# Three tiles of their own for the modulation weights during the output projection of a hybrid mLSTM/GDN block

## The chip, the cores and the metric

The kernel runs on one NeuronCore of a Trainium2 chip. The metric is the device time of one execution in microseconds (us). TensorE is the matrix engine (PE in the profile, its weight loads PEld), VectorE is DVE, ScalarE is ACT, GpSimd is POOL, and SyncE (SP) issues most of the transfers from HBM.

## The reference

One encoder layer on 256 tokens of width 2048, in float32. Only the middle of it matters here:

```
mod = silu(c) @ ada_w + ada_b            # 6 vectors of 2048: shift/scale/gate for mixer and FFN
h   = rms_norm(x) * (1 + scale_m) + shift_m
...                                       # mLSTM branch y_a, gated delta rule branch y_b
x   = x + gate_m * ((g_a * y_a + g_b * y_b) @ w_out)        # the output projection
hf  = rms_norm(x) * (1 + scale_f) + shift_f
gt, up = split(hf @ w_gate_up)
x   = x + gate_f * ((silu(gt) * up) @ w_down)
return rms_norm(x)
```

`w_out` is 2048 x 2048 (16 MiB). `ada_w` is 2048 x 12288, six parts of 16 MiB. Part 4 (`scale_f`) has to be known before the FFN's input can be made, part 5 (`gate_f`) only at the very end.

## The kernel before

Everything is one instruction stream per engine, scheduled ahead of time; an engine runs its instructions in that order, and waits on semaphores for what an instruction needs. The instructions of SP are DMA issues, and an issue that waits holds up all issues behind it.

Weights stream in as tiles of 1 MiB (128 partitions x 8 KB). `tjob` (line 167) is the worker of a dense product: for each of its chunks `u` it takes a tile `raw_...` and loads it (line 177), and then, in two halves of two 128-row blocks each, ACT rounds it into `wh` (line 180), DVE subtracts to get the remainder `wl` (line 181), and TensorE does twelve matmuls of 128x512 per half: eight with `wh` (lines 198 and 199) and four with `wl` (line 201). `wh` and `wl` have three buffers each, so DVE and ACT can be up to three halves ahead of TensorE.

The output projection is four jobs `o0` to `o3` of four chunks each, 32 halves in all, at the loop on lines 1122 to 1139. Names read so: `raw_o1_2` is chunk 2 of job o1, `wl_o1_2_0` the remainder of its first half. After each job `residual` (line 1080) multiplies the two result tiles by `gm` (line 1083), adds them to `x1` (line 1084) and squares them for the norm (line 1085). `gm` itself is made at the start of the stage by `row` (line 1066): DVE builds diagonal tiles `dg` (line 1072), TensorE multiplies them with ones (line 1074), ACT copies the result (line 1075). The stage before is the job `ya3` of `y_a`, whose end adds into `mg` (line 1003) and transposes it into `mgh`/`mgl` (lines 1009 and 242). `x1` is loaded with 2 MiB from ACT's queue at the start of the stage (line 1064).

The modulation vectors are not matmuls. `ada_part` (line 118) is a generator: each step takes a tile `ada{part}_{b}`, loads 1 MiB of `ada_w` into it (line 123) and lets DVE multiply it with the broadcast `silu(c)` and sum it up (line 124). The steps are laid in between other work as `background`; `sums()` advances it by one step. In the output projection the steps of part 4 from `ada4_3` to `ada4_15` are taken: 13 tiles.

Pools: `st` lives through the whole program. Its tag `raw` has three buffers of 8 KB, and both the weights' tiles (line 176) and the `ada` tiles (line 122) take their turns in it: a load into one of them waits until the last reader of the tile three turns earlier is done, which for a weight tile is its second `wl` (line 181) and for an `ada` tile its sum (line 124). `wp` (line 1062) is a pool that lives only in the output projection; it holds `gm`, `dg` and the residual's `tm`, in memory that the pool `ml` of the stages before has given back and that `ffh`/`ffl` of the FFN take afterwards.

Of the kernel before, what the change touches and what calls it, by code (L numbers as in the profile page):

```python
# [9 lines left out]
F32 = mybir.dt.float32  # L10
# [5 lines left out]
P = 128  # L16
T = 256
D = 2048
# [34 lines left out]
def hybrid_block(ctx: ExitStack, tc: tile.TileContext, xr, nfr, crow, pk_d, cst_d, ada2, ada4, win0, winb, wint, wba, wbb, wo, wgu, wd, out, dbg=None):  # L53
# [3 lines left out]
    def pool(stack, name, bufs=1, **kw):  # L57
        return stack.enter_context(tc.tile_pool(name=name, bufs=bufs, **kw))

    cp = pool(ctx, "cp")  # L60
    st = pool(ctx, "st")
# [53 lines left out]
        order(S.activation(row_c[:, g * 512 : (g + 1) * 512], pc_, AF.Silu))  # L115


    def ada_part(part, row_c):

        c0 = part * KB  # L120
        for b in range(KB):
            raw = st.tile([P, D], F32, tag="raw", bufs=3, name=f"ada{part}_{b}")
            nc.sync.dma_start(raw, ada4[part - 2, b])
            V.scalar_tensor_tensor(raw, raw, 1.0, row_c[:, :D], ALU.mult, ALU.mult, accum_out=mod[:, c0 + b : c0 + b + 1])  # L124
            yield True
        V.tensor_tensor(mod[:, c0 : c0 + KB], mod[:, c0 : c0 + KB], pk[:, PK_ADAB + c0 : PK_ADAB + c0 + KB], ALU.add)
        yield True
# [312 lines left out]
    with ExitStack() as s0:  # L440
# [18 lines left out]
        def loads(b):  # L459
            ra = [w0.tile([P, D + 2], F32, tag="ra", bufs=5, name=f"ra{b}_{i}") for i in range(2)]  # L460
            raw = st.tile([P, N0, P], F32, tag="raw", bufs=3, name=f"raw0_{b}")
            for i in range(2):
                order(nc.sync.dma_start(ra[i], ada2[b, :, i]))
            order(nc.sync.dma_start(raw, win0[b]))
            return ra, raw
# [10 lines left out]
        ra, raw = loads(0)  # L476
# [18 lines left out]
        for b in range(KB):  # L495
            if b:
                ra, raw = loads(b)
# [347 lines left out]
    for part in (2, 3, 4):  # L845
        background.append(ada_part(part, row_c))
# [213 lines left out]
    sd.close()  # L1060
    xp = pool(ctx, "xp", side="right")
    wp = pool(sw, "wp")
    x1 = xp.tile([P, 2, D], F32, name="x1")
    S.dma_start(x1, xr)

# [74 lines left out]
    if dbg is not None and "x1" in dbg:  # L1140
        G.dma_start(dbg["x1"], x1)
    background.append(ada_part(5, row_c))
    sw.close()
    sc.close()
    pool(ctx, "edgeF").tile([P, 56], F32, name="edgeF")
# [61 lines left out]
    for j in range(FB // 4):  # L1207
# [4 lines left out]
        for e2 in range(2):  # L1212
            px = gps(f"pxf{j}_{e2}")
            for e in range(2):
                f = 2 * e2 + e
                for t in range(2):
                    PE.transpose(px[:, e * T + t * P : e * T + (t + 1) * P], sg[:, t, f * P : (f + 1) * P], ident)
            b = 4 * j + 2 * e2
# [143 lines left out]
```

## Time and profile before

| | us |
|---|---|
| median of three runs | 2047.38 (2047.14 to 2054.85) |
| the profiled execution, its own time | 2052.6 |
| its span, first to last instruction | 2050.5 |
| TensorE busy | 1963.4 (96% of the span) |
| DVE busy | 1394.8 (68%) |
| ACT busy | 1047.7 (51%) |
| stage of the output projection, first matmul of o0 to the start of the last half of o3 | 1220.09 to 1321.84 |

All starts are in us from the span's beginning. A matmul's busy time is its latency, and matmuls overlap in the array, so where TensorE keeps up is read from the distance of their starts and not from busy time. A row of the timeline ends, in brackets, with how long its engine sat idle before it and what ended that. In the rows of waits the three numbers are us in total, times, and the longest.

### The profile page before, as it was taken

To read this page: it belongs to the slowest core of one execution; us is meant where nothing else is said; L and a number is where in the kernel's file an instruction comes from. 1 tells how busy PE (TensorE), PEld (TensorE's weight loads), DVE (VectorE), ACT (ScalarE), POOL (GpSimd) and SP (SyncE) were. 2 spreads that over 40 slices of the span, in tenths; PEclk is the share of its full clock that TensorE was granted. 3 is DMA by queue.
4 is the path that set the end of the run, shared out by engine and by line. 5 is a ranking of instruction groups with operands and counts; after the bars stand their busy time and mean duration, and the time that the engine had idled before them with its cause. 6 is when DMAs were issued, how large, how long until landed. Compare 5 with 4: busy or idle time off the path is not lost.

```text
span 2050.5 us, 27063 instructions
## 1 busy us (share of the span) xinstructions
PE 1963.4 (96%) x10374; PEld 1711.0 (83%) x10374; DVE 1394.8 (68%) x2059; ACT 1047.7 (51%) x1582; POOL 106.4 (5%) x205
## 2 busy tenths in 40 slices
PE   8999999999999899999999998899999999999998
PEld 6887879988989788889878887678888888888886
DVE  5788776777888588765667777766656665555554
ACT  3147548755774667556443443464444444444443
POOL 0002210110101011101100000000000000000000
PEclk9999999999999999999999999999999999999999
DMA  9986664556667565766986677756766766555553
GB/s 400 420 323 214 194 202 155 179 183 226 235 216 227 180 214 213 236 234 248 368 298 229 218 261 286 279 189 242 259 236 253 254 230 225 197 204 201 202 203 142
DMA packets 78962, 485.64 MB, mean 237 GB/s; under 512 B 10585, under 2 KB 15969, under 8 KB 24433
## 3 DMA queue, kind: packets, MB, share of 16 engines
q1 hardware_dynamic: 63360, 450.95, 60.6%
q0 software_dynamic: 8160, 17.88, 3.8%
q10 hardware_dynamic: 7314, 15.10, 1.9%
q8 instruction: 81, 1.33, 0.3%
q14 instruction: 47, 0.39, 0.1%
HBM read 467.07 MB, written 16.82 MB: 236 GB/s over the span
## 4 chain that ended last, share of the span: by engine, by line
PE 67%; DVE 13%; DMA 11%; ACT 6%; issue 3%; POOL 1%; ACTq 0%; SPq 0%; DVEq 0%; POOLq 0%
PE acc_b L159 4%; PE acc_up L199 4%; PE acc_up L201 4%; PE acc_up L198 4%; PE acc_d L199 4%; PE acc_d L201 4%; PE acc_d L198 4%; PE acc_gt L199 4%; PE acc_gt L201 3%; PE acc_gt L198 3%; DMA ra<-ada 3%; PE acc_b L161 2%; DMA ada<-ada 1%; PE acc_yb L199 1%; PE acc_yb L201 1%
## 5 line engine op out<-in xcount | busy, mean ns | idle before, releaser
L181 DVE TENSOR_TENSOR wl_d<-raw_d,wh_d 128x1024 fp32r<-128x1024 f32 x88 | 107.5, 1225 | 105.3 <-ACT wh_d L180 103.1
L181 DVE TENSOR_TENSOR wl_up<-raw_up,wh_up 128x1024 fp32r<-128x1024 f32 x88 | 107.6, 1225 | 100.0 <-ACT wh_up L180 100.0
L124 DVE SCALAR_TENSOR_TENSOR ada<-ada,crow 128x2048 f32<-128x2048 f32 x64 | 146.4, 2287 | 19.5 <-DMA ada<-ada 19.4
L180 ACT ACTIVATE wh_d<-raw_d 128x1024 fp32r<-128x1024 f32 x88 | 92.9, 1056 | 124.5 <-PE acc_d L199 114.3
L181 DVE TENSOR_TENSOR wl_gt<-raw_gt,wh_gt 128x1024 fp32r<-128x1024 f32 x88 | 107.7, 1224 | 70.1 <-ACT wh_gt L180 68.6
L180 ACT ACTIVATE wh_up<-raw_up 128x1024 fp32r<-128x1024 f32 x88 | 92.9, 1056 | 119.9 <-PE acc_up L199 71.6
L159 PE MATMUL acc_b<-hh,wh_b 128*128 128x256 f32 x576 | 141.4, 288 | 9.3 <-ACT wh_b L155 7.7
L180 ACT ACTIVATE wh_gt<-raw_gt 128x1024 fp32r<-128x1024 f32 x88 | 92.9, 1055 | 108.7 <-PE acc_gt L199 61.3
L159 PE MATMUL acc_b<-hl,wh_b 128*128 128x256 f32 x576 | 138.9, 284 | 0.0
L199 PE MATMUL acc_gt<-wh_gt,hfl 128*128 128x512 f32 x352 | 136.3, 387 | 0.1
L198 PE MATMUL acc_gt<-wh_gt,hfh 128*128 128x512 f32 x352 | 135.2, 384 | 0.0
L199 PE MATMUL acc_up<-wh_up,hfl 128*128 128x512 f32 x352 | 133.6, 379 | 0.0
L198 PE MATMUL acc_up<-wh_up,hfh 128*128 128x512 f32 x352 | 133.5, 379 | 0.0
L198 PE MATMUL acc_d<-wh_d,ffh 128*128 128x512 f32 x344 | 130.8, 380 | 0.0
L199 PE MATMUL acc_d<-wh_d,ffl 128*128 128x512 f32 x344 | 130.7, 380 | 0.0
L159 PEld LDWEIGHTS acc_b<-hh,wh_b 128*128 128x128 f32 x576 | 114.4, 199 | 10.1 <-ACT wh_b L155 8.4
L509 PE MATMUL first<-x,raw 128*128 128x256 f32 x512 | 114.5, 382 | 7.7 <-ACT x L502 7.7
L509 PEld LDWEIGHTS first<-x,raw 128*128 128x128 f32 x512 | 96.2, 190 | 26.0 <-ACT x L502 13.7
L159 PEld LDWEIGHTS acc_b<-hl,wh_b 128*128 128x128 f32 x576 | 114.4, 199 | 0.0
L180 ACT ACTIVATE wh_o<-raw_o 128x1024 fp32r<-128x1024 f32 x64 | 66.2, 1054 | 77.1 <-DMA raw_o<-wo 44.9
L298 DVE SCALAR_TENSOR_TENSOR cv<-pad,pk,cv 128x256 f32<-128x256 f32 x192 | 90.8, 481 | 19.2 <-ACT cv L296 17.1
L156 DVE TENSOR_TENSOR wl_b<-raw_b,wh_b 128x1024 fp32r<-128x1024 f32 x72 | 86.8, 1219 | 24.6 <-ACT wh_b L155 24.2
(369 smaller groups left out, 5031.5 us busy)
## 6 DMA issues: line engine op xcount, KB each, us to landing
ada<-ada SPq DMA_DIRECT2D x64, 1024.0 KB, 4.9
raw_gt<-wgu SPq DMA_DIRECT2D x44, 1024.0 KB, 5.0
raw_up<-wgu SPq DMA_DIRECT2D x44, 1024.0 KB, 5.0
raw_d<-wd SPq DMA_DIRECT2D x44, 1024.0 KB, 4.9
raw_b<-winb SPq DMA_DIRECT2D x36, 1024.0 KB, 5.1
ra<-ada SPq DMA_DIRECT2D x32, 1025.0 KB, 15.7
raw<-win SPq DMA_DIRECT2D x16, 1024.0 KB, 14.5
raw_z<-wint SPq DMA_DIRECT2D x16, 1024.0 KB, 5.1
```

Of the source, the lines that this page charges most:

```text
L124: V.scalar_tensor_tensor(raw, raw, 1.0, row_c[:, :D], ALU.mult, ALU.mult, accum_out=mod[:, c0 + b : c0 + b + 1])
L156: V.tensor_tensor(wl, raw[:, k0 : k0 + 8], wh.bitcast(F32), ALU.subtract)
L159: PE.matmul(o, wh[:, k], both(x, k0 + k).rearrange("p a b -> p b a"), start=k0 + k + i == 0, stop=False)
L161: PE.matmul(o, wl[:, k], both(hh, k0 + k).rearrange("p a b -> p b a"), start=False, stop=k0 + k == KB - 1)
L180: order(S.activation(wh, raws[u][:, k0 : k0 + 2], AF.Copy), early)
L181: order(V.tensor_tensor(wl, raws[u][:, k0 : k0 + 2], wh.bitcast(F32), ALU.subtract), early)
L198: order(PE.matmul(ps[t], tok(xh, kk, t), turns(wh[:, k]), start=kk == 0, stop=False), early and steps > 1)
L199: PE.matmul(ps[t], tok(xl, kk, t), turns(wh[:, k]), start=False, stop=False)
L201: PE.matmul(ps[t], tok(xh, kk, t), turns(wl[:, k]), start=False, stop=kk == last)
L298: V.scalar_tensor_tensor(cv, pd[:, i : i + T], w[i], cv, ALU.mult, ALU.add)
L509: PE.matmul(first[o], raw[:, o], x[:, b], start=b == 0 and o % 2 == 0, stop=b == KB - 1 and o % 2 == 1)
```

## The change

`ada_part` no longer names its pool, tag and number of buffers, but reads them from a list of three. The list says `st`, `raw`, 3 as before, except from the opening of `wp` to its closing, where it says `wp`, `ada`, 3.

```
+    ada_in = [st, "raw", 3]
+
     def ada_part(part, row_c):
...
-            raw = st.tile([P, D], F32, tag="raw", bufs=3, name=f"ada{part}_{b}")
+            raw = ada_in[0].tile([P, D], F32, tag=ada_in[1], bufs=ada_in[2], name=f"ada{part}_{b}")
...
     wp = pool(sw, "wp")
+    ada_in[:] = [wp, "ada", 3]
     x1 = xp.tile([P, 2, D], F32, name="x1")
...
     background.append(ada_part(5, row_c))
+    ada_in[:] = [st, "raw", 3]
     sw.close()
```

The numbers of instructions on each engine stay the same. The scheduler lays some of them in another order, all of it between the end of `ya3` and the start of `o3`; POOL's order does not change. The three new tiles lie in memory that `ml` used (for `mkq`, `vt`, `sgo`, `bc` and `mdec`), and the first load into them, `ada4_3`, now waits for the last addition into `mg` of job `ya3` (line 1003); the next two loads wait for nothing more.

SP at the start of the output projection, before (the number behind a name is the buffer's):

```order
L177 DMA raw_o0_2_10908<-wo 128x2048
L123 DMA ada4_3_10926<-ada4 128x2048
L177 DMA raw_o0_3_10945<-wo 128x2048
L123 DMA ada4_4_10963<-ada4 128x2048
L123 DMA ada4_5_10990<-ada4 128x2048
L177 DMA raw_o1_0_10995<-wo 128x2048
L123 DMA ada4_6_11029<-ada4 128x2048
```

SP at the same place, now (line numbers are two higher here):

```order
L179 DMA raw_o0_2_10908<-wo 128x2048
L179 DMA raw_o0_3_10945<-wo 128x2048
L125 DMA ada4_3_10926<-ada4 128x2048
L125 DMA ada4_4_10963<-ada4 128x2048
L125 DMA ada4_5_10990<-ada4 128x2048
L179 DMA raw_o1_0_10995<-wo 128x2048
L125 DMA ada4_6_11029<-ada4 128x2048
```

`raw_o0_3` went ahead of `ada4_3`. From `raw_o1_0` on, the order of issues is that of before (a weight tile, an `ada` tile in turn); what an issue waits for is another tile.

DVE around the end of job o0, before (L181 makes `wl`, L124 sums an `ada` tile, L1083 and L1084 are the residual):

```order
L181 TENSOR_TENSOR wl_o0_3_2_10967<-raw_o0_3_10945,wh_o0_3_2_10966 128x1024
L124 SCALAR_TENSOR_TENSOR ada4_5_10990,mod_85<-ada4_5_10990,crow_73 128x2048
L181 TENSOR_TENSOR wl_o1_0_0_10998<-raw_o1_0_10995,wh_o1_0_0_10997 128x1024
L1083 TENSOR_TENSOR tmss1_10835_0_0_10982<-acc_o0_0_10838,gm_10802 128x512
L1083 TENSOR_TENSOR tmss1_10835_1_0_10986<-acc_o0_1_10839,gm_10802 128x512
L1084 TENSOR_TENSOR x1_10800<-x1_10800,tmss1_10835_0_0_10982 128x512
L1084 TENSOR_TENSOR x1_10800<-x1_10800,tmss1_10835_1_0_10986 128x512
L181 TENSOR_TENSOR wl_o1_0_2_11014<-raw_o1_0_10995,wh_o1_0_2_11013 128x1024
L124 SCALAR_TENSOR_TENSOR ada4_6_11029,mod_85<-ada4_6_11029,crow_73 128x2048
L181 TENSOR_TENSOR wl_o1_1_0_11035<-raw_o1_1_11032,wh_o1_1_0_11034 128x1024
```

DVE at the same place, now (line numbers are two to three higher):

```order
L183 TENSOR_TENSOR wl_o0_3_2_10967<-raw_o0_3_10945,wh_o0_3_2_10966 128x1024
L126 SCALAR_TENSOR_TENSOR ada4_6_11029,mod_85<-ada4_6_11029,crow_73 128x2048
L183 TENSOR_TENSOR wl_o1_0_0_10998<-raw_o1_0_10995,wh_o1_0_0_10997 128x1024
L183 TENSOR_TENSOR wl_o1_0_2_11014<-raw_o1_0_10995,wh_o1_0_2_11013 128x1024
L1086 TENSOR_TENSOR tmss1_10835_0_0_10982<-acc_o0_0_10838,gm_10802 128x512
L1086 TENSOR_TENSOR tmss1_10835_1_0_10986<-acc_o0_1_10839,gm_10802 128x512
L1087 TENSOR_TENSOR x1_10800<-x1_10800,tmss1_10835_0_0_10982 128x512
L1087 TENSOR_TENSOR x1_10800<-x1_10800,tmss1_10835_1_0_10986 128x512
L183 TENSOR_TENSOR wl_o1_1_0_11035<-raw_o1_1_11032,wh_o1_1_0_11034 128x1024
L126 SCALAR_TENSOR_TENSOR ada4_7_11050,mod_85<-ada4_7_11050,crow_73 128x2048
```

The residual of o0 now stands behind both `wl` of the next job's first chunk and not behind one; the sums of the `ada` tiles stand one step earlier. At the end of o1 it stands behind two `wl` where it stood behind none, and at the end of o2 behind one where it stood behind none. Near the start of the stage the sum of `ada4_3` moved behind the diagonals `dg2_2`, `dg2_3` and both `mgl`; it now stands right ahead of `wl_o0_1_2`.

More of the change, by code (lines that the diff above doesn't have):

```diff
@@ L115, in c_row @@
         order(S.activation(row_c[:, g * 512 : (g + 1) * 512], pc_, AF.Silu))
+    ada_in = [st, "raw", 3]
     def ada_part(part, row_c):
@@ L121, in ada_part @@
         for b in range(KB):
-            raw = st.tile([P, D], F32, tag="raw", bufs=3, name=f"ada{part}_{b}")
+            raw = ada_in[0].tile([P, D], F32, tag=ada_in[1], bufs=ada_in[2], name=f"ada{part}_{b}")
             nc.sync.dma_start(raw, ada4[part - 2, b])
@@ L1062, in hybrid_block @@
     wp = pool(sw, "wp")
+    ada_in[:] = [wp, "ada", 3]
     x1 = xp.tile([P, 2, D], F32, name="x1")
@@ L1142, in hybrid_block @@
     background.append(ada_part(5, row_c))
+    ada_in[:] = [st, "raw", 3]
     sw.close()
```

## The prediction

> **What bounds the kernel now.** I read the page's busy times first, then the stage in question by windows, then its waits, then TensorE's and DVE's timelines. TensorE leads over the whole program and two thirds of the chain that ends last run on it:
>
> ```profile
> PE 1963.4 (96%) x10374; PEld 1711.0 (83%) x10374; DVE 1394.8 (68%) x2059; ACT 1047.7 (51%) x1582; POOL 106.4 (5%) x205
> PE 67%; DVE 13%; DMA 11%; ACT 6%; issue 3%; POOL 1%; ACTq 0%; SPq 0%; DVEq 0%; POOLq 0%
> ```
>
> So a transfer or a DVE wait costs time only where TensorE runs dry. Three windows (the columns are length, busy times of PE, PEld, DVE, ACT, POOL, granted clock, DMA share, GB/s): a stretch near the start in which transfers are queued deep, the last stretch of `ya3`, and the output projection.
>
> ```profile
> 25.00:50.00 25.00, 22.97 (x105) 19.30 (x104) 16.28 (x18) 3.21 (x8) 0.00 (x0) 1.00 1.01 420
> 1201.69:1220.09 18.40, 18.40 (x87) 16.12 (x86) 9.99 (x11) 7.80 (x9) 0.00 (x0) 1.00 0.49 171
> 1223.50:1321.50 98.00, 86.59 (x370) 70.70 (x369) 76.33 (x89) 37.22 (x49) 0.00 (x0) 0.97 0.84 313
> ```
>
> `ya3` keeps TensorE full; the output projection does not, although none of DVE, ACT and the DMA engines is full either. Who waits there (stretch 1200 to 1325, then SP's own waits in 1180 to 1330):
>
> ```profile
> ACT wh_o L180 <- DMA raw_o<-wo: 44.9, 10, 8.5
> PE acc_o L198 <- ACT wh_o L180: 8.2, 5, 3.5
> PE acc_o L201 <- DVE wl_o L181: 3.2, 3, 1.8
> ...
> SPq L123 <- DVE wl_o L181: 46.9, 13, 8.1
> SPq L177 <- DVE ada L124: 34.4, 13, 8.0
> ```
>
> This is a loop through the shared ring of three tiles: a weight tile's load is held until DVE has summed an `ada` tile (13 times), the `ada` load until DVE has made a `wl` (13 times), and then ACT waits ten times for a weight tile that was issued too late. TensorE's timeline gives what this costs. Starts of halves, and the gaps in them:
>
> ```profile
> 1220.09 0.38 PE L198 MATMUL acc_o<-wh_o,mgh 128*128 128x512 f32 x1
> ...
> 1232.70 0.38 PE L198 MATMUL acc_o<-wh_o,mgh 128*128 128x512 f32 x1
> ...
> 1235.29 0.38 PE L198 MATMUL acc_o<-wh_o,mgh 128*128 128x512 f32 x1
> ...
> 1254.32 0.38 PE L198 MATMUL acc_o<-wh_o,mgh 128*128 128x512 f32 x1
> ...
> 1260.60 0.80 PE L198 MATMUL acc_o<-wh_o,mgh 128*128 128x512 f32 x1 [3.53 <-ACT wh_o L180]
> ...
> 1265.89 0.63 PE L198 MATMUL acc_o<-wh_o,mgh 128*128 128x512 f32 x1
> ...
> 1268.83 0.38 PE L198 MATMUL acc_o<-wh_o,mgh 128*128 128x512 f32 x1
> ...
> 1277.67 1.13 PE L201 MATMUL acc_o<-wl_o,mgh 128*128 128x512 f32 x4 [1.77 <-DVE wl_o L181]
> ...
> 1288.78 0.48 PE L198 MATMUL acc_o<-wh_o,mgh 128*128 128x512 f32 x1 [2.21 <-ACT wh_o L180]
> ...
> 1313.97 0.48 PE L198 MATMUL acc_o<-wh_o,mgh 128*128 128x512 f32 x1 [1.69 <-ACT wh_o L180]
> ...
> 1321.84 0.38 PE L218 MATMUL acc_o<-wh_o,mgh 128*128 128x512 f32 x1
> ```
>
> A half that waits for nothing takes 1235.29 - 1232.70 = 2.59. The first three halves hold the transposes and `row`'s matmuls besides (12.61, of which 3 x 2.59 = 7.77, so 4.84 of other work, which stays). From 1232.70 to 1321.84 lie 28 halves: 89.14 against 28 x 2.59 = 72.52. **The stage loses 16.6 us**, and that is the most the change can win there. The largest piece is one event: the half at 1254.32 takes 6.28 (3.69 too long), the next, after 3.53 idle, 5.29 and the one after 2.94, since its matmuls start 0.43 apart instead of 0.22 for a while. That is 6.7 of the 16.6.
>
> The half clock after a gap: row first, 5.29 + 2.94 - 2 x 2.59 = 3.05 lost after the wait itself. The Trainium skill, "TensorE: Matmul & The Clock Gate", section "What's actually happening", has the clock come back after one busy window of about 3.4 us; by it the loss would be an estimated 1.7 and the stage's 15.3. The row decides.
>
> **The change, part by part.** Removed: the ring's sharing. A weight load then waits only for the second `wl` of the weight tile three before it, an `ada` load for the sum of the `ada` tile three before. Take chunk 2 of o1, whose late arrival made the gap at 1260.60. SP and DVE there:
>
> ```profile
> 1252.19 0.33 SPq L177 DMA_DIRECT2D raw_o<-wo  x1
> ...
> 1235.71 1.23 DVE L181 TENSOR_TENSOR wl_o<-raw_o,wh_o 128x1024 fp32r<-128x1024 f32 x1 [1.31 <-ACT wh_o L180]
> 1236.85 2.29 DVE L124 SCALAR_TENSOR_TENSOR ada<-ada,crow 128x2048 f32<-128x2048 f32 x1
> 1239.07 1.22 DVE L181 TENSOR_TENSOR wl_o<-raw_o,wh_o 128x1024 fp32r<-128x1024 f32 x1
> ```
>
> Its load went out at 1252.19, held by an `ada` sum, 4.7 before the half that needs it could have begun (1254.32 + 2.59 = 1256.9). In the new order it waits for the last `wl` of o0, which DVE started at 1239.07 and which one more `ada` sum now precedes: 1239.07 + 1.14 + 2.21 = 1242.4, some 10 us earlier than before and 14 ahead of that half. A landing takes 4.9 to 6.0 (below), so the wait is covered. The same holds for each later chunk, since the ring is now three weight tiles deep instead of one and a half.
>
> Added, price one: **transfers**. Same count and bytes, but packed closer.
>
> ```profile
> ada<-ada SPq DMA_DIRECT2D x64, 1024.0 KB, 4.9
> raw_o<-wo SPq DMA_DIRECT2D x16, 1024.0 KB, 6.0
> x<-xr ACTq DMA_DIRECT2D x1, 2048.0 KB, 9.2
> ...
> 1219.18 0.33 SPq L123 DMA_DIRECT2D ada<-ada  x1
> ```
>
> From 1219.18 on, 13 weight tiles, 13 `ada` tiles and 2 MiB of `x1` must land: 28 MiB, 29.4 MB. One tile at the 420 GB/s of the first window is 2.5, so 4.9 means 2.4 of fixed time, and bytes flow from 1221.6. Without stalls the last two halves start at 1302.63 (1321.84 - 16.62 - 2.59) and need both `wl` 1.73 (8 x 0.216) later, at 1304.4; less two `wl` (1.14 each) and one `wh` (1.05) the last weight tile must have landed by 1301.0. That is 79.4 for 29.4 MB, 370 GB/s. At 420 it takes 70: hidden, with 9 to spare. Ends: nothing at 420, and 14.5 late at 313 (94), the mean of this stage, which I do not take as a limit since the loop above held the issues back.
>
> Price two: **the burst at the start**. `raw_o0_3` takes the place at 1219.18; `ada4_3` now waits for the last addition into `mg`, and DVE stands still for it if it lands late, with `wl_o0_1_2` right behind it.
>
> ```profile
> 1221.28 1.29 DVE L1003 TENSOR_TENSOR mg<-mg,gta 128x512 f32<-128x512 f32 x2
> 1222.48 1.22 DVE L181 TENSOR_TENSOR wl_o<-raw_o,wh_o 128x1024 fp32r<-128x1024 f32 x1
> 1223.62 1.65 DVE L1072 TENSOR_SCALAR dg<-cst,mod 128x128 f32<-128x128 f32 x8
> 1225.19 2.28 DVE L124 SCALAR_TENSOR_TENSOR ada<-ada,crow 128x2048 f32<-128x2048 f32 x1
> ```
>
> The addition ends at 1222.6, so the three `ada` loads go out there. `ada4_3` lands at 1227.5 if alone (4.9) and at 1221.6 + 4 x 2.5 = 1231.6 if all of `raw_o0_3` and `x1` goes first. Then 2.21 for the sum and 1.14 for `wl_o0_1_2`: 1230.9 to 1235.0. TensorE asks for it 1.73 into its half at 1232.70, at 1234.4. Price 0 to 0.6; I take 0.6. No weight load suffers behind it on SP, as the next, `raw_o1_0`, waits for `wl_o0_1_2` anyway and is needed only five halves later. The early issue of `row`'s matmuls moves work inside the 4.84.
>
> Price three: **DVE**, which had idle time that hid its sums. Four rows in a row, around the end of o2:
>
> ```profile
> 1299.68 1.29 DVE L1083 TENSOR_TENSOR tmss<-acc_o,gm 128x512 f32<-128x512 f32 x2 [0.72 <-PE acc_o L201]
> 1300.88 1.28 DVE L1084 TENSOR_TENSOR x<-x,tmss 128x512 f32<-128x512 f32 x2
> 1302.08 2.35 DVE L181 TENSOR_TENSOR wl_o<-raw_o,wh_o 128x1024 fp32r<-128x1024 f32 x2
> 1304.35 2.29 DVE L124 SCALAR_TENSOR_TENSOR ada<-ada,crow 128x2048 f32<-128x2048 f32 x1
> ```
>
> By their starts a residual is 2.40, two `wl` 2.27, and a sum 2.21 (the `wl` behind that at 1236.85 starts at 1239.07). From 1223.62: `dg` twice 1.57, `mgl` 1.2, 13 sums 28.7, 29 `wl` 32.9, three residuals 7.2: 73.1, ending at 1296.8 against 1304.4. It fits, but the residual of o2 cannot start before TensorE ends o2, ideally at 1287.1 (1220.09 + 4.84 + 24 x 2.59). Behind it come `wl`, sum, `wl`: 1287.1 + 2.40 + 1.14 + 2.21 + 1.14 = 1294.0, and TensorE wants that `wl` at 1294.0 (1287.1 + 2 x 2.59 + 1.73). Just on time, so every delay there is passed on: 0 to 0.5, I take 0.5.
>
> Sum: 16.6 - 0.6 - 0.5 = 15.5 at best. In the old stage each piece stood between two larger ones and could not be seen alone; for hand-overs of the kind of 0.1 to 0.6 between ACT, DVE and TensorE I leave 1.5. **Gain 14.0.** Behind the stage all work hangs on its end and moves up with it. The part-5 sums use the shared ring again as before, and the new tiles' memory is first overwritten by `ffl` after the first `up` job, long after they were read. The profiled execution took 2052.6 (span 2050.5), 5.2 above the median of 2047.4; the stage's loss is taken to be the same in both: 2047.4 - 14.0 = 2033.4.
>
> **The rivals.** *Transfers become the limit.* For it: the stage already moves 313 GB/s, the sum needs 370. Against it: 420 in the first window. At 350 the 29.4 MB take 84, the last tile is 4.6 late and the gain is 16.6 - 4.6 = 12.0; at 313 it is 2, no change. The Trainium skill's "DMA: Bandwidth & Descriptors", section "Where 436 GB/s comes from", lets the HBM side bind at about 358 GB/s for one core; by it the last tile would be an estimated 2.7 late and the gain at most 13.9. The 420 of this trace speaks against a limit there.
>
> *The change is slower.* One mechanism: with two rings the `ada` loads take turns with the weight loads on the same DMA engines, and the mixed stream runs slower than either. It decides below 277 GB/s: then 29.4 MB take 106.2, the last tile is 26.8 late, 10.2 more than the 16.6 lost now, and the time is above 2057. Against it: 313 here with gaps in it, in the same mix.
>
> *DVE takes over the waits.* Its order is fixed; if an `ada` tile lands late in the middle of the stage, all `wl` behind it are late. For it: DVE has 7.6 of slack in the whole stage and none at the end of o2. If each of the three job ends costs 2 and the start 2, the gain is 8.6: 2038.8. *Nothing happens*: if TensorE's gaps came from DVE's fixed order and not from late tiles, they would stay; against it stand ACT's 44.9 behind transfers.
>
> **How the numbers follow.** Forecast (11 to 16.6 won, 2031 to 2036.5): 0.66. DVE takes over part (5 to 11 won): 0.18, a quarter of it above the bound. Transfers limit or nothing happens (within 5): 0.12. Slower: 0.04. The bound is 0.5%, 10.2 us, about what this measurement tells from no change: faster 0.71, same 0.25, slower 0.04. The range 2030 to 2040.5 holds the forecast and half of the second case.
>
> **What would show it.** Right: ACT's wait for `raw_o` falls from 44.9 below 10; no gap of TensorE in the stage above 1; granted clock 1.00 in it; first to last half 85 to 88 instead of 101.75; DMA rate there above 350. Wrong: DVE rows with idle time ended by `ada` transfers; halves still longer than 2.59 in o1 and o2; or a gain in the stage that the FFN's start, from 1322 on, gives back.

## The result, and the profile after

The changed kernel takes 2035.18 us (median of four, 2032.23 to 2036.88) against 2051.11 (2047.14 to 2056.65) of the kernel before in the same rounds: a ratio of 0.9915, with a 95% interval from 0.9898 to 0.9931. The forecast was 2033.4, a ratio of 0.993 to the 2047.4 it started from. The profiled execution has a span of 2035.0 (time 2036.88) against 2050.5, so 15.5 less. Of all executions below, one, of the own ring of two, ran in a slower state (granted clock 0.751, 2528.75 us) and is left out of its median.

Windows of the kernel after: the output projection, from the first matmul of o0 to the start of the last half of o3, and 20 us in the middle of it. The columns are those of the prediction's windows.

```profile
1218.40:1305.90 87.50, 85.51 (x390) 72.15 (x388) 78.79 (x93) 38.92 (x50) 0.00 (x0) 1.00 0.92 366
1270.00:1290.00 20.00, 20.00 (x95) 17.50 (x94) 17.97 (x20) 8.22 (x11) 0.00 (x0) 1.00 1.01 412
```

The stage now lasts 87.48 where it lasted 101.75: 14.27 won. The granted clock is back at 1.00, the DMA engines move 366 GB/s over the stage and 412 where both rings run freely. Another 1.67 of the span's 15.5 come from ahead of the stage (it starts at 1218.42 instead of 1220.09), where the two kernels compute the same, and what follows the stage took 0.4 longer. In the ten profiles of this study, which compute the same up to there, the start lies anywhere from 1216.19 to 1222.06. That wander, of some 6 us, is why small differences below are read from the stage and not from the time.

Waits of ACT and DVE (stretch 1200 to 1312), and SP's own (1180 to 1312):

```profile
ACT wh_o L182 <- PE acc_o L201: 16.4, 14, 1.8
...
ACT wh_o L182 <- DMA raw_o<-wo: 8.7, 5, 2.7
...
DVE ada L126 <- DMA ada<-ada: 4.3, 1, 4.3
```

```profile
SPq L179 <- DVE wl_o L183: 69.3, 16, 12.4
...
SPq L125 <- DVE ada L126: 5.4, 3, 1.8
...
SPq L179 <- DVE ada L126: 1.8, 1, 1.8
```

The loop is cut. ACT's wait for weight tiles fell from 44.9 to 8.7, and what it now waits for most often is TensorE, which has become the slower one. SP still waits 79.6 in total (95.7 before, both without the 29.9 of `ya3`'s loads), but a weight load now waits for a `wl`; the one wait for an `ada` sum that is left, 1.8, lies ahead of the stage. DVE, which before waited 1.7 for three `ada` tiles together, now stands 4.3 for a single one. TensorE's timeline shows what that costs, and where the other late half is:

```profile
1218.42 0.38 PE L200 MATMUL acc_o<-wh_o,mgh 128*128 128x512 f32 x1
...
1230.91 0.38 PE L200 MATMUL acc_o<-wh_o,mgh 128*128 128x512 f32 x1
...
1234.79 1.13 PE L203 MATMUL acc_o<-wl_o,mgh 128*128 128x512 f32 x4 [1.99 <-DVE wl_o L183]
1235.76 0.38 PE L200 MATMUL acc_o<-wh_o,mgh 128*128 128x512 f32 x1
...
1292.74 0.38 PE L200 MATMUL acc_o<-wh_o,mgh 128*128 128x512 f32 x1
...
1295.54 0.38 PE L200 MATMUL acc_o<-wh_o,mgh 128*128 128x512 f32 x1
...
1305.90 0.38 PE L220 MATMUL acc_o<-wh_o,mgh 128*128 128x512 f32 x1
...
1312.03 1.57 PE L1173 MATMUL pxn<-cst,xn 128*128 128x128 f32 x8 [3.38 <-ACT xn L1166]
```

Without waits the stage would take 31 x 2.59 + 4.84 = 85.13; it takes 87.48. Of the 2.35 left, 2.26 are the half from 1230.91 to 1235.76 (4.85 instead of 2.59), and 0.21 the half from 1292.74 to 1295.54, chunk 1 of o3; the first three halves with their other work took 0.12 less than before (12.49 instead of 12.61). All others take 2.59. At the stage's end nothing is given back: the FFN's first transposes (`pxn`) start 6.13 after the last half's start, as before (1321.84 to 1327.97), after the same 3.38 idle. The row of before:

```profile
1327.97 1.30 PE L1169 MATMUL pxn<-cst,xn 128*128 128x128 f32 x5 [3.38 <-ACT xn L1162]
```

DVE and SP at the two places:

```profile
1225.70 1.28 DVE L244 TENSOR_TENSOR mgl<-pxm,mgh 128x512 fp32r<-128x512 f32 x2
1231.30 2.29 DVE L126 SCALAR_TENSOR_TENSOR ada<-ada,crow 128x2048 f32<-128x2048 f32 x1 [4.32 <-DMA ada<-ada]
...
1287.54 1.29 DVE L1086 TENSOR_TENSOR tmss<-acc_o,gm 128x512 f32<-128x512 f32 x2 [2.03 <-PE acc_o L203]
```

```profile
1220.96 1.28 SPq L125 DMA_DIRECT2D ada<-ada  x3
...
1243.73 0.33 SPq L179 DMA_DIRECT2D raw_o<-wo  x1
```

`ada4_3`, issued at 1220.96, landed shortly before 1231.30, and `wl_o0_1_2` stands behind its sum. The second is the end of o2: the residual waits for TensorE, and a `wl` and a sum follow it before the `wl` of chunk 1 of o3.

### The profile page after: what moved, and what is told of

Read it like the earlier page. It is cut to its first block, busy times and chain, and to the rows that moved or that the text cites. A ratio compares the mean times of both kernels' runs of the same rounds, so it can differ in the third digit from the quotient of the medians.

```text
span 2035.0 us, 27065 instructions
## 1 busy us (share of the span) xinstructions
PE 1956.7 (96%) x10374; PEld 1706.4 (84%) x10374; DVE 1394.1 (69%) x2059; ACT 1050.0 (52%) x1582; POOL 106.4 (5%) x205
## 4 chain that ended last, share of the span: by engine, by line
PE 70%; DMA 11%; DVE 9%; ACT 6%; issue 2%; POOL 1%; ACTq 0%; SPq 0%; DVEq 0%; POOLq 0%
PE acc_up L200 4%; PE acc_up L203 4%; PE acc_up L201 4%; PE acc_d L201 4%; PE acc_d L200 4%; PE acc_d L203 4%; PE acc_gt L201 4%; PE acc_gt L200 4%; PE acc_gt L203 4%; PE acc_b L161 3%; DMA ra<-ada 3%; DMA ada<-ada 2%; PE acc_o L203 2%; PE acc_o L200 2%; PE acc_o L201 2%
```

## The experiments

Theory: the loss was a loop through the shared ring, and three further tiles take it away. Rivals: what helped was the new order of instructions; or the separation of the two kinds of tile, rather than their number; or the stage is now held by DVE's sums. Besides, two things were open: what made `ada4_3` late, and whether three is the right number.

### The old sharing put back, in a new order (mix3)

```
+    raw_in = [st, "raw", 3]
...
-                raws[u] = st.tile([P, 4, 512], F32, tag="raw", bufs=3, name=f"raw_{name}_{u}")
+                q = raw_in if name in ("o1", "o2", "o3") else [st, "raw", 3]
+                raws[u] = q[0].tile([P, 4, 512], F32, tag=q[1], bufs=q[2], name=f"raw_{name}_{u}")
...
+    raw_in[:] = [wp, "ada", 3]
```

> The ada tiles and the weight tiles of o1 to o3 share one ring of three again, but in the new pool's memory; the order on DVE and TensorE in the first half of the stage is that of the changed kernel. Theory (a weight load held by an ada sum is what starved the stage): it starves again, first to last half 97 to 104 us instead of 87.5, time 2042 to 2054. Rival (the new order of DVE, with the residual behind the next wl, is what helped): first to last half 86 to 90, time 2032 to 2038.

Measured: 2050.73, a ratio of 0.9997 (0.9977 to 1.0017) to 2051.86 of the kernel before, and a stage of 101.34. Its first and last half, and the waits in it, ACT's and then SP's:

```profile
1218.47 0.38 PE L202 MATMUL acc_o<-wh_o,mgh 128*128 128x512 f32 x1
...
1319.81 0.38 PE L222 MATMUL acc_o<-wh_o,mgh 128*128 128x512 f32 x1
```

```profile
ACT wh_o L184 <- DMA raw_o<-wo: 27.0, 7, 7.9
```

```profile
SPq L181 <- DVE ada L127: 32.8, 11, 10.5
SPq L126 <- DVE wl_o L185: 30.3, 8, 5.7
```

Weight loads wait for `ada` sums and `ada` loads for `wl` again, and the gain is gone, though the tiles lie in the new pool's memory.

The order is not quite held fixed in this run, since the scheduler lays the instructions anew for each sharing. By the starts in the traces, DVE's order in mix3 is that of the kernel after only up to the `wl` behind the third `ada` sum. What separates order from sharing is the own ring of two (below): its DVE order is that of mix3 up to the residual of o0 and the `wl` behind it. Yet it loses next to nothing in o1 (0.04), where mix3 loses 4.1 in three halves. So the order on DVE up to there neither makes nor takes the gain; that the later differences of order do nothing is not shown apart from the sharing.

### One shared ring of six (mix6)

```
-    raw_in[:] = [wp, "ada", 3]
+    raw_in[:] = [wp, "ada", 6]
```

(as mix3, and the `ada` tiles' list with the same 6.)

> One shared ring for the ada tiles and the weight tiles of o1 to o3, but of six tiles. Theory in its form 'depth' (six tiles in flight, whoever holds them): first to last half 86.5 to 89, time 2032 to 2038, as with three and three. Rival 'separation' (a weight load must not wait for a sum at all): the stalls come back in part, first to last half above 92, time above 2040.

Measured: 2036.32, a ratio of 0.9932 (0.991 to 0.9954), and a stage of 87.06, with two late halves, at the same two places as in the kernel after: 1.84 and 0.21. Its first and last half, and SP's largest wait between them (1216 to 1304):

```profile
1216.19 0.38 PE L202 MATMUL acc_o<-wh_o,mgh 128*128 128x512 f32 x1
...
1303.25 0.38 PE L222 MATMUL acc_o<-wh_o,mgh 128*128 128x512 f32 x1
```

```profile
SPq L181 <- DVE ada L127: 26.8, 7, 5.4
```

So the separation is not needed. Seven loads are still held by an `ada` sum, 26.8 in all, and yet ACT has no wait for a weight tile of this stage left: the hold ends early enough. What counts is how many tiles there are before a load has to wait for a reader.

### A shared ring of four, own rings of two and of five (mix4, own2, own5)

```
-    raw_in[:] = [wp, "ada", 3]
+    raw_in[:] = [wp, "ada", 4]
```

(as mix3, and the `ada` tiles' list with the same 4.)

> One shared ring of four tiles for the ada tiles and the weight tiles of o1 to o3 (three gave a stage of 101.3, six 87.1). Theory (a weight tile turns over in about one landing plus two halves, and two weight tiles in flight are just enough): the stage lies between, 88 to 95, time 2035 to 2043. Rival (any sharing of fewer than six starves it): above 97.

```
-    ada_in[:] = [wp, "ada", 3]
+    ada_in[:] = [wp, "ada", 2]
```

> The ada tiles have a pool of their own with two tiles instead of three. Theory (the weights' ring of three is what counts, and two ada tiles cover one landing of 5 us behind one sum of 2.2 at a pace of one sum per 5.2): as with three, first to last half 87 to 89.5, the FFN's start not later, time 2032 to 2039. Rival (as with one tile, the sums fall behind): the FFN's first matmul is late by 3 us or more, time above 2040.

and the same line with 5:

> The ada tiles have a pool of their own with five tiles; the order on the engines is that of the changed kernel. Theory (three already cover every sum): first to last half 87 to 88, ada4_3 lands as late as before (10 to 11 us), nothing won. Rival (the longer burst at the start delays the weight loads behind it): 89 or more.

Measured, against 2050.55 of the kernel before: four shared tiles 2042.95, a ratio of 0.9965 (0.9949 to 0.9981), a stage of 89.68; own ring of two 2038.50 (nine runs), a ratio of 0.9949 (0.9933 to 0.9966), a stage of 88.46; own ring of five 2034.67 in one run, a stage of 87.23. ACT's wait for weight tiles, in the ring of four and in the own ring of two (both from 1200 to the stage's end):

```profile
ACT wh_o L184 <- DMA raw_o<-wo: 24.8, 8, 5.6
```

```profile
ACT wh_o L182 <- DMA raw_o<-wo: 27.0, 9, 5.1
```

By the stage, each from one profiled execution, against the 85.13 without waits, three shared tiles lose 16.2, four 4.6, an own ring of two 3.3, three 2.35, five 2.1, six shared 1.9. Nearly all is won by the fourth tile; own tiles beyond three bring 0.25 at most. Besides the start, the late halves of four and of two lie around the beginnings of o2 and o3, 0.75 to 2.04 each. They are few for the 25 to 27 that ACT waits: ACT and DVE can be up to three halves ahead, so most of that wait need not reach TensorE. The time of the ring of four is 4 us longer than its stage says (2050.55 - 12.07 = 2038.5); its profiled stage also began 3.6 later than that of the kernel after, in the part that is the same. What that is beyond the wander named above I don't know.

### An own ring of one (own1)

```
-    ada_in[:] = [wp, "ada", 3]
+    ada_in[:] = [wp, "ada", 1]
```

> The ada tiles have a pool of their own with one tile instead of three. Theory: weight loads are still free, but each ada load now waits for the sum before it and takes about 5 us more, so the sums fall behind and the last of them land after the last residual: first to last half 86 to 92, but the wait from the end of o3 to the FFN's first matmul grows by 10 us or more; time 2042 to 2060. Rival (only being out of the weights' ring matters): time 2032 to 2038.

Measured: 2060.29, 0.3 above the expected range, and a ratio of 1.0043 (1.0028 to 1.0057) to 2051.86: slower, though its stage takes 89.47, 12.3 less than before. The loss is behind the stage:

```profile
1331.47 2.29 DVE L126 SCALAR_TENSOR_TENSOR ada<-ada,crow 128x2048 f32<-128x2048 f32 x1 [4.98 <-DMA ada<-ada]
...
1334.29 0.99 DVE L1179 TENSOR_SCALAR hf<-pxn,affn,mod 128x256 f32<-128x256 f32 x2
```

```profile
1316.73 1.97 PE L1173 MATMUL pxn<-cst,xn 128*128 128x128 f32 x8 [6.09 <-ACT xn L1166]
1335.34 0.79 PE L200 MATMUL acc_gt<-wh_gt,hfh 128*128 128x512 f32 x1 [16.64 <-ACT hfh L1180]
```

Each load waits for the sum ahead of it, so the last three sums come after o3's residual, with DVE idle for a landing before two of them, and the FFN's input `hf` needs all of part 4. TensorE stands 16.64 there, and `pxn` comes 2.7 later than in the kernel after: 19.4 given back for 12.3 won.

### Without the sums (nosums)

```
-            if i in ((4, 6, 7), (1, 2, 4, 6), (1, 2, 4, 6), (1, 2, 4))[g]:
-                sums()
...
-                sums(P)
+                background.clear()
+                V.memset(mod[:, 4 * KB + 3 : 5 * KB], 0.0)
```

> Leaves out the 13 part-4 sums and their loads in the output projection (their values are set to zero), so no ada traffic and no sums on DVE there. Theory (what is left to win in the changed kernel is the 2.3 at the start and 0.2 at o3): first to last half 85.0 to 85.7 (31 x 2.59 and 4.84), time 2 to 3 us below the changed kernel. Rival (transfers or DVE still cost time that does not show as gaps): 83 or less, or more than 5 us won.

Measured: 2033.75, a ratio of 0.992 (0.9895 to 0.9945), a stage of 85.02 in which no half is late.

```profile
1218.30:1303.30 85.00, 85.00 (x390) 72.48 (x389) 52.02 (x66) 38.96 (x50) 0.00 (x0) 1.00 0.63 220
```

This is the floor, and it confirms the 16.6 that the prediction put on the loop: 101.75 - 85.02 = 16.73. Leaving out all 13 loads and sums would win only 2.5 more in the stage than the change did. DVE is down from 78.79 to 52.02 busy and the transfers from 366 to 220 GB/s, so neither holds the changed stage by more than these 2.5.

### `x1` loaded later (x1late)

```
-    S.dma_start(x1, xr)
...
+    S.activation(x1[:, 0, 0:1], gm[:, D - 1 : D], AF.Copy)
+    S.dma_start(x1, xr)
```

The one-element copy into `x1` makes the load wait until `gm` is complete.

> The changed kernel, but the 2 MiB load of x1 goes out only when gm is complete (one element of x1 is written from gm first, and the load overwrites it). The scheduler also puts the sum of ada4_3 two wl later. Theory (the 2.3 us left at the start come from ada4_3's load sharing the DMA engines with x1's): ada4_3 lands in 5 to 7.5 us instead of 10.3, no gap of TensorE ahead of o0's chunk 2, first to last half 85.0 to 85.6, time about 2 us below the changed kernel (2031 to 2035). Rival (the landing is slow for itself, by the three ada loads in a row): it still lands after 10 us.

Measured: 2035.98, a ratio of 0.9926 (0.9911 to 0.9942) to 2050.55, and a stage of 86.18, both above what was expected. The first of the three `ada` loads, issued at 1221.00 here and at 1220.96 in the kernel after, by its issue and landing (KB and us; first the kernel after, then this one):

```profile
ada<-ada SPq DMA_DIRECT2D x1, 1024.0 KB, 10.3
```

```profile
ada<-ada SPq DMA_DIRECT2D x1, 1024.0 KB, 5.4
...
x<-xr ACTq DMA_DIRECT2D x1, 2048.0 KB, 12.0
```

The two other `ada` loads go out behind it in both, so they are not what made it late; the ring of one says the same, since there no other `ada` load goes out and `ada4_3` still takes 10.8. It was `x1`, issued 2.3 us earlier on ACT's queue. With `x1` at 1229.78 the late half at the start is gone, but not by the landing alone, since DVE's order changed too:

```profile
1224.77 1.22 DVE L183 TENSOR_TENSOR wl_o<-raw_o,wh_o 128x1024 fp32r<-128x1024 f32 x1
...
1227.47 1.22 DVE L183 TENSOR_TENSOR wl_o<-raw_o,wh_o 128x1024 fp32r<-128x1024 f32 x1
1228.61 2.29 DVE L126 SCALAR_TENSOR_TENSOR ada<-ada,crow 128x2048 f32<-128x2048 f32 x1
```

The first of these is `wl_o0_1_2`, the tile of the late half, and here it stands ahead of the sum of `ada4_3`. What the earlier landing would have won in the old order was not measured. In place of that half, ACT waits for a weight tile in o1, behind which a half is 0.82 late:

```profile
1247.49 2.01 ACT L182 ACTIVATE wh_o<-raw_o 128x1024 fp32r<-128x1024 f32 x2 [5.65 <-DMA raw_o<-wo]
```

```profile
1251.66 0.48 PE L203 MATMUL acc_o<-wl_o,mgh 128*128 128x512 f32 x1 [0.55 <-DVE wl_o L183]
```

That weight tile, chunk 1 of o1, was issued at 1236.49, behind `x1` and two `ada` loads (from 1230.93), and took 10.9 to land, where the same tile took 7.4 in the kernel after. So the 2 MiB seem to collide still, with something that has more cover; which of the loads ahead of it does it was not taken apart. Against the kernel after the stage is 1.30 shorter, which is less than these times can tell: 15 won here against its own kernel before, 16 won by the change against its own.

## Why the prediction was right

**The bound and its mechanism** were right. The loop between weight and `ada` tiles is shown by mix3 (the sharing put back, the gain gone) together with the own ring of two (the same order on DVE up to the beginning of o1, and no loss in o1), and its size by the floor: 16.73 measured, 16.6 forecast. What the prediction called the ring's sharing is, by mix6, its depth: its own phrase "three weight tiles deep instead of one and a half" is the part that held, as six shared tiles do as well as three and three. A weight load that waits for an `ada` sum is then no harm in itself.

**The half clock** went with the gaps: 0.97 before, 1.00 after. The ring of three in its new order has it twice, each time for one half, here after a gap of 1.99:

```profile
1258.02 0.48 PE L202 MATMUL acc_o<-wh_o,mgh 128*128 128x512 f32 x1 [1.99 <-ACT wh_o L184]
...
1259.22 0.63 PE L202 MATMUL acc_o<-wh_o,mgh 128*128 128x512 f32 x1
1259.64 0.63 PE L203 MATMUL acc_o<-wh_o,mgl 128*128 128x512 f32 x1
...
1262.40 0.38 PE L202 MATMUL acc_o<-wh_o,mgh 128*128 128x512 f32 x1
```

The half takes 4.38, 1.79 too long, with starts 0.43 apart for about 3.6 us. This is close to the 1.7 estimated from the one busy window of the Trainium skill's "TensorE: Matmul & The Clock Gate", section "What's actually happening"; the row of before, 3.05, was a longer case. For the sum it made no difference, since both sizes lie inside the 16.6.

**Chunk 2 of o1** was issued at 1243.73, 8.5 before the 1252.19 of the kernel before. With the stage's earlier start of 1.67 the forecast 1242.4 is 1240.7 here, so it came 3.0 later than worked out. DVE works without a pause from the late sum at 1231.30 up to the `wl` that this load waits for, so it is the late `ada4_3` that shows here too. The load landed in 5.7, with 12.7 of cover.

**Transfers** were rightly priced at nothing. The mix of both kinds runs at 412 GB/s over 20 us, so the rival at 350 and the one that needs less than 277 both fall, and so does, for one core alone, the 358 that the Trainium skill's "DMA: Bandwidth & Descriptors", section "Where 436 GB/s comes from", gives. The landings did get longer with the rate: before, 6.6 for a weight tile and 5.2 for an `ada` tile at 304 GB/s (1235 to 1300); after, at 396 (1235 to 1290), 7.4 and 9.7. The same medians of the kernel after over 1232 to 1306:

```profile
raw_o<-wo SPq DMA_DIRECT2D x12, 1024.0 KB, 7.4
ada<-ada SPq DMA_DIRECT2D x10, 1024.0 KB, 9.7
```

The 4.9 to 6.0 that the prediction used for a landing came from the kernel before, with its gaps. It had found 14 of cover for chunk 2 of o1, so it did not matter; a tile with only 6 of cover would have been late at the median of 7.4.

**The burst at the start** is the step that failed: 2.26 and not 0 to 0.6. The term took its upper end, a landing at 1231.6, or 1229.9 with the earlier start of the stage; it came at 1231.3, and these 1.4 on top of 0.6 are most of the 2.26. So the case was the right one, since x1late shows that `x1` ahead of it costs this load 4.9 (10.3 against 5.4), and the bound was too low: the working had the load landed as soon as 4 MiB could have moved at 420. In the ring of one the bytes are indeed through by about 1229, and the load still lands at 1231.8 (last section). An estimate that fits is the landing without `x1` ahead, 5.4, plus 5.0 for 2 MiB at 420: 10.4, where 10.3 was measured. The sign "no gap above 1" failed here for the same reason, and the row that was to show a wrong forecast, DVE idle until an `ada` transfer, did appear, once.

**DVE at the end of o2** was right in place and size: 0.21 in the half that it named, with 0 to 0.5 forecast. The rival "DVE takes over the waits" put 2 at each job's end; the others show none.

**The 1.5 for hand-overs** was not needed: no other half is late. It cancelled the error at the start, so the forecast of 14.0 came close to the 14.27 of the stage partly by luck: 1.66 too little was taken off for the start, 1.5 and 0.3 too much for hand-overs and the end of o2, and the first three halves took 0.12 less. The time of 2033.4 is near by luck in part as well: the medians lie 15.9 apart, 1.9 more than forecast, and that of the kernel before came out 3.7 above the 2047.4 that the sum started from.

**Nothing is given back at the stage's end**: 6.13 from the last half to the FFN, before and after. That this could have gone otherwise is shown by the ring of one.

## What to carry to other kernels

Two streams in one ring of buffers tie each one's loads to the other's reader, and then the ring's depth for each is half of its number; count how many tiles there are between a load's issue and its use, and compare that with the landing time of a full queue, not of an empty one. Giving the streams rings of their own and making one ring deeper are the same remedy; here the fourth shared tile brought 11.7 us, and the fifth and sixth together 2.6. When many small stalls go at once, price the first load behind a large transfer by that transfer's whole time and a landing of its own besides (here 5.0 and 5.4), and look at what must be finished by the end of the stage: a ring that is too shallow can save the stage and lose more behind it.

## What the runs showed that I had not expected

- A gap of 1.99 us put TensorE at half clock in the ring of three (above), while gaps of 2.21 and 1.77 in the kernel before and of 1.99 in the kernel after did not. In the ring of one a gap of 2.46 did, and the half behind it took 1.60 too long:

```profile
1235.26 1.25 PE L203 MATMUL acc_o<-wl_o,mgh 128*128 128x512 f32 x4 [2.46 <-DVE wl_o L183]
1236.31 0.63 PE L200 MATMUL acc_o<-wh_o,mgh 128*128 128x512 f32 x1
1236.73 0.63 PE L201 MATMUL acc_o<-wh_o,mgl 128*128 128x512 f32 x1
```

The length of one gap does not decide it here; what else does was not tried.
- In the ring of one, `ada4_3` lands at about 1231.8, though the DMA engines have almost nothing left to do from 1229 to 1232:

```profile
DMA packets 20, 0.07 MB, mean 25 GB/s; under 512 B 13, under 2 KB 13, under 8 KB 13
```

The last five packets of 8 KB on SP's queue, which carries no other load then, come one after another, some 0.3 us apart, from 1229.7 to 1231.0, when the bytes ahead of them are through. Why was not tried; here it is part of what makes 1 MiB behind 2 MiB take longer than the rate says.
